# Products of seven-product row-tile pairs interleaved with those of the next pair, in a hybrid attention and FFN block

## The chip, the core and the metric

The kernel runs on one core of a Trainium2 chip. Its engines run side by side, each in the order of its own instruction list: PE (matrix multiply, into PSUM), DVE (elementwise), ACT (elementwise and activation functions), POOL (little used here) and SP, whose list here holds nothing but DMA issues. They meet at semaphores only. The metric is the device time of one execution in microseconds; less is better. The kernel before takes 1153.43 us, the median of three executions (1153.13, 1153.43, 1155.93).

## The reference

One transformer block over 256 positions of width 2048, all in float32. Four kinds of token mixing share one input projection; then comes the feed-forward part, which the change is about:

```python
h = rms_norm(x, norm_mix_pre)
mix = hybrid_mixer(h, ...)                 # retention, SSD scan, two attentions
x = x + rms_norm(mix @ w_out, norm_mix_post)
h = rms_norm(x, norm_ffn_pre)
f = (jax.nn.silu(h @ w_gate) * (h @ w_up)) @ w_down      # 2048 -> 5632 -> 2048
x = x + rms_norm(f, norm_ffn_post)
```

## The kernel before

Float32 precision is had from a fast PE format by splitting each operand in two: `hi` is the operand rounded (an ACT cast, L767) and `lo` what is left (a DVE subtraction, L768). One product is then three matmuls of 128 x 128 by 128 x 512: hi by hi, hi by lo, lo by hi (`mm1`, L811 to L815; the line of a matmul tells which of the three it is). Activations are split once and stay in SBUF; weights stream in from HBM, and every 128 x 1024 piece of them costs one ACT cast and one DVE subtraction.

The feed-forward part has three stages. The first (`gemm`) computes the first 512 hidden columns in the plain way. The second, called the gate stage below, computes the other 10 blocks of 512 columns of `w_gate` and `w_up` together. The third, the down stage, does `w_down` in two passes q = 0 and 1, each with 22 units. A unit is a pair of row tiles of the weights (2 x 128 rows): in the gate stage 8 units make a block. A unit has a 2 x 2 arrangement of weights (a, b for the two column groups, rows 0 and 1) against a 2 x 2 arrangement of activations (two row tiles, two halves of the 256 positions). Plainly it takes eight products (`eight`). `seven` does it in seven by a Strassen-like scheme: it needs sums of the weights, `ta` (L824, 128 x 1024) and `tb` (L826 and L827, 128 x 512 each), and sums of the activations, made once and held (`cmb`). So a seven-product unit costs PE 21 matmuls in place of 24, and costs DVE and ACT more: its four weight operands are `w0` (as loaded), `wa` (from ta), `wc` (half a piece as loaded) and `wb` (from tb). `S_UNITS` and `S_DOWN` say which units are taken in seven: 3 of 8 in each gate block, 4 of 22 and 7 of 22 in the down stage. Each such unit is done whole before the next unit begins.

Results gather in PSUM, which has 8 banks: four in one pool (`ps_a`: m1, q5, m7, m6) and two and two in others (b2 and b3; b4 and b8). `sums` folds the four into two SBUF tiles when the last seven of a block is done, and `join` (L860 to L864) adds the other four at the block's end. Then ACT and DVE make silu(g) * v (L928, L929), the block of f. `turn` transposes it on PE (eight 128 x 128 transposes) and ACT copies it to SBUF (L897); `hidden` splits it for the down stage (tiles `fs`, and `cmb` for a unit taken in seven).

A scheduler reorders each engine's list when the program is built; the lists are fixed before the run. What paces them is in the pools: weights as loaded live in 5 buffers (`raw`, 512 KB each), their split parts in 4 `hi` and 4 `lo` buffers. SP issues a load when the buffer that it reuses has been read for the last time, and the loads stand in one list, so a late one holds up those behind it.

Of the kernel before, what the change touches and what calls it, by code (L numbers as in the profile page):

```python
# [33 lines left out]
CK = 2  # L34
FFB = FF // 512
FKT = FF // P

S_UNITS = (0, 2, 4)
S_DOWN = ((0, 1, 5, 8), (0, 1, 3, 5, 7, 8, 10))
X_STEPS = [(0, 1), (1, 2), (2, 4), (4, 6), (6, 8), (8, 10), (10, 12), (12, 14), (14, 16)]  # L40


# [21 lines left out]
def _pack4(wa, wb, blocks, n_kt):  # L64


    parts = []
    for (ca, cb, n) in blocks:
        a, b = (w[:, c:c + n].reshape(n_kt // 2, 2, P, n) for w, c in ((wa, ca), (wb, cb)))
        q = np.stack([a[:, 0], b[:, 1], b[:, 0], a[:, 1]], axis=2)  # L70
        parts.append(np.ascontiguousarray(q).reshape(-1))
    return np.concatenate(parts)

# [26 lines left out]
def block_kernel(ctx: ExitStack, tc: tile.TileContext, I, out):  # L100
# [15 lines left out]
    def T(shape, name, dt=F32):  # L116

        count["t"] += 1
        return big.tile(shape, dt, tag="t", name=f"{name}_{count['t']}")
# [662 lines left out]
        split_to(o[:, 0], o[:, 1], s)  # L782
        return o

    def load4(src, i):

        n = 4 * P * 512
        w = src[i * n:(i + 1) * n].rearrange("(p c n) -> p c n", p=P, c=4)
        out = []
        for k in range(2):  # L790
            raw = wp.tile([P, CK * 512], F32, tag="raw", bufs=5, name="raw")
            r3 = raw.rearrange("p (c n) -> p c n", c=CK)
            nc.sync.dma_start(r3, w[:, 2 * k:2 * k + 2, :])
# [26 lines left out]
    def seven(m, src, i, x, u, cmb, last):  # L820

        ad, bc_ = load4(src, i)
# [8 lines left out]
        s = lambda j: [cmb[:, i, j, :] for i in range(2)]  # L831
        for name, (xa, xb), (hi, lo), k in (
                ("m1", xpart(x, u, 0, 0), w0, 0), ("b3", s(3), w0, 1), ("q5", s(0), wa, 0), ("m7", s(2), wa, 1),
                ("b2", xpart(x, u, 1, 0), wc, 0), ("m6", s(1), wb, 0), ("b4", xpart(x, u, 1, 1), wb, 1)):
            mm1(m, name, xa, xb, hi[:, k, :], lo[:, k, :], last and name[0] != "b")

    def eight(m, src, i, x, u, last=False, halves=(0, 1), ws=None):

        if ws is None:
            ws = [split_new(v) for v in load4(src, i)]  # L840
        (w0, w1) = ws
        for h in halves:
            for name, k, (hi, lo), j in (("b2" if h == 0 else "b4", 0, w0, 0), ("b3" if h == 0 else "b8", 1, w0, 1),
                                         ("b3" if h == 0 else "b8", 0, w1, 0), ("b2" if h == 0 else "b4", 1, w1, 1)):
                end = last and (name, j) in (("b3", 0), ("b8", 0), ("b2", 1), ("b4", 1)) and w1 is ws[1] and j + k == (
                    0 if name in ("b3", "b8") else 2)
                mm1(m, name, *xpart(x, u, k, h), hi[:, j, :], lo[:, j, :], end)
        return ws
# [19 lines left out]
    def combine_hs(u):  # L868
# [6 lines left out]
    accs = [[accps(f"ff{h}{i}") for i in range(2)] for h in range(2)]  # L875
    gemm(hs, [I["w_g"], I["w_u"]], [fr[0], fr[0]], 512, KT, accs, 4, (2, 3, 4, 7),
         {1: lambda: gained(1, 0), 2: lambda: gained(1, 1), 3: lambda: gained(1, 2), 4: lambda: gained(1, 3),
          5: lambda: [x_norm(h) for h in range(2)], 6: lambda: combine_hs(S_UNITS[0]),
          8: lambda: combine_hs(S_UNITS[1]), 9: lambda: combine_hs(S_UNITS[2])})
    for h in range(2):  # L880
        spill(h)
    sg = []
# [7 lines left out]
    def turn(b, f):  # L890

        ft.append(T([P, 4, S], f"ft{b}"))
        for h in range(2):
            ps = ps_c.tile([P, 512], F32, tag="b", name=f"fT{b}{h}")
# [15 lines left out]
    for b in range(1, FFB):  # L910
        m = {}
        g, v = T([P, 2, 512], "g"), T([P, 2, 512], "v")
        for u in range(KT // CK):
            i = (b - 1) * (KT // CK) + u
            if u in S_UNITS:
                seven(m, I["w_gu"], i, hs, u, cmb[u], u == S_UNITS[-1])
            else:
                eight(m, I["w_gu"], i, hs, u, u == KT // CK - 1)
            if u == 0:
                turn(b - 1, f)  # L920
            if u == S_UNITS[-1] + 1:
# [13 lines left out]
    for q in range(2):  # L935
# [103 lines left out]
```

## Time and profile before

| | |
|---|---|
| median of three executions | 1153.43 us |
| the profiled execution | 1157.54 us |
| its span on the core | 1155.6 us |
| PE busy in the span | 1123.8 us, 97% |
| DVE busy | 865.6 us, 75% |
| ACT busy | 613.1 us, 53% |
| granted TensorE clock, mean of the span | 0.996 |
| HBM, mean of the span | 193 GB/s |

The span is what the trace covers; the execution has 1.9 us around it. A matmul's duration in the trace is its time through the pipeline (0.39 us), while the next one starts after 0.23 us; so PE's busy share counts overlaps once, hides a short pause, and says little on how near PE is to its pace. The distance between the starts of matmuls tells that. For DVE and ACT too, a row's duration is a little longer than the distance to the next start. In a row of the timeline, the bracket at the end has the engine's idle time just before the instruction and what ended it.

### The profile page before, as it was taken

To read this page: it belongs to the slowest core of one execution; us is meant where nothing else is said; L and a number is where in the kernel's file an instruction comes from. 1 tells how busy PE (TensorE), PEld (TensorE's weight loads), DVE (VectorE), ACT (ScalarE), POOL (GpSimd) and SP (SyncE) were. 2 spreads that over 40 slices of the span, in tenths; PEclk is the share of its full clock that TensorE was granted. 3 is DMA by queue.
4 is the path that set the end of the run, shared out by engine and by line. 5 is a ranking of instruction groups with operands and counts; after the bars stand their busy time and mean duration, and the time that the engine had idled before them with its cause. 6 is when DMAs were issued, how large, how long until landed. Compare 5 with 4: busy or idle time off the path is not lost. (4 is left out here: it accounts for less than half of the span.)

```text
span 1155.6 us, 14581 instructions
## 1 busy us (share of the span) xinstructions
PE 1123.8 (97%) x5341; PEld 928.8 (80%) x5341; DVE 865.6 (75%) x1185; ACT 613.1 (53%) x846; POOL 14.2 (1%) x37
## 2 busy tenths in 40 slices
PE   9999999999999999999999999999999999989996
PEld 7787888888888887887787787787788788868885
DVE  5556647777565577898898897887898988479845
ACT  6644435565444475655555555555565666355532
POOL 0000000000000010000000000000000000000000
PEclk9999999999999999999999999999999999999998
DMA  8964454564456676556556556456456556546654
GB/s 275 317 227 146 142 155 124 185 208 162 153 188 192 213 266 204 182 195 205 181 186 204 176 196 204 164 199 206 164 196 215 192 194 218 194 153 216 221 196 150
DMA packets 65447, 224.35 MB, mean 194 GB/s; under 512 B 8032, under 2 KB 8544, under 8 KB 65376
## 3 DMA queue, kind: packets, MB, share of 16 engines
q1 hardware_dynamic: 65232, 223.42, 57.9%
q8 instruction: 42, 0.69, 0.2%
q14 instruction: 29, 0.24, 0.1%
q10 hardware_dynamic: 144, 0.01, 0.0%
HBM read 219.20 MB, written 4.19 MB: 193 GB/s over the span
## 5 line engine op out<-in xcount | busy, mean ns | idle before, releaser
L767 ACT CAST hi<-raw 128x1024 fp32r<-128x1024 f32 x248 | 238.6, 980 | 205.9 <-PE b L815 180.8
L768 DVE TENSOR_TENSOR lo<-raw,hi 128x1024 fp32r<-128x1024 f32 x248 | 277.6, 1133 | 67.4 <-ACT hi L767 63.5
L182 DVE TENSOR_TENSOR lo<-raw,hi 128x1024 fp32r<-128x1024 f32 (+3 forms) x154 | 175.5, 1154 | 115.9 <-ACT hi L181 115.4
L181 ACT CAST hi<-raw 128x1024 fp32r<-128x1024 f32 (+3 forms) x154 | 150.7, 994 | 129.9 <-PE wo L199 32.1
L814 PE MATMUL b<-lo,hs 128*128 128x512 f32 x460 | 180.3, 392 | 0.3 <-DVE lo L768 0.3
L813 PE MATMUL b<-hi,hs 128*128 128x512 f32 x460 | 180.1, 392 | 0.0
L815 PE MATMUL b<-hi,hs 128*128 128x512 f32 x460 | 179.2, 390 | 0.0
L814 PE MATMUL b<-lo,fs 128*128 128x512 f32 x286 | 111.7, 391 | 0.3 <-DVE lo L768 0.3
L815 PE MATMUL b<-hi,fs 128*128 128x512 f32 x286 | 111.4, 390 | 0.0
L813 PE MATMUL b<-hi,fs 128*128 128x512 f32 x286 | 110.7, 390 | 0.1
L814 PEld LDWEIGHTS b<-lo,hs 128*128 128x128 f32 x460 | 86.4, 188 | 18.4 <-DVE lo L768 1.0
L813 PEld LDWEIGHTS b<-hi,hs 128*128 128x128 f32 x460 | 86.4, 188 | 17.8
L815 PEld LDWEIGHTS b<-hi,hs 128*128 128x128 f32 x460 | 86.4, 188 | 17.6
L824 DVE TENSOR_TENSOR ta<-raw 128x1024 f32<-128x1024 f32 x41 | 50.1, 1223 | 30.6 <-DMA raw<-in_w_gu 29.2
L814 PEld LDWEIGHTS b<-lo,fs 128*128 128x128 f32 x286 | 53.8, 188 | 12.6 <-DVE lo L768 1.4
L813 PEld LDWEIGHTS b<-hi,fs 128*128 128x128 f32 x286 | 53.7, 188 | 11.9 <-ACT hi L767 0.7
L768 DVE TENSOR_TENSOR lo<-tb,hi 128x1024 fp32r<-128x1024 f32 x41 | 50.1, 1222 | 17.1 <-ACT hi L767 17.1
L815 PEld LDWEIGHTS b<-hi,fs 128*128 128x128 f32 x286 | 53.8, 188 | 11.1
L767 ACT CAST hi<-tb 128x1024 fp32r<-128x1024 f32 x41 | 43.1, 1052 | 28.9 <-DVE lo L768 13.0
L767 ACT CAST hi<-ta 128x1024 fp32r<-128x1024 f32 x41 | 43.2, 1054 | 26.0 <-PE b L815 17.4
L768 DVE TENSOR_TENSOR lo<-ta,hi 128x1024 fp32r<-128x1024 f32 x41 | 50.0, 1219 | 0.1
L196 PE MATMUL wo<-hi,ms 128*128 128x512 f32 x128 | 50.0, 390 | 0.0
(378 smaller groups left out, 2025.8 us busy)
## 6 DMA issues: line engine op xcount, KB each, us to landing
raw<-in_w_gu SPq DMA_DIRECT2D x160, 512.0 KB, 4.5
raw<-in_w_down SPq DMA_DIRECT2D x88, 512.0 KB, 4.2
raw<-in_w_in SPq DMA_DIRECT2D x78, 512.0 KB, 4.5
raw<-in_w_out SPq DMA_DIRECT2D x32, 512.0 KB, 3.5
raw<-in_w_in SPq DMA_DIRECT2D x16, 384.0 KB, 3.1
raw<-in_w_g SPq DMA_DIRECT2D x8, 512.0 KB, 4.8
raw<-in_w_u SPq DMA_DIRECT2D x8, 512.0 KB, 4.7
raw<-in_w_in SPq DMA_DIRECT2D x8, 264.0 KB, 2.8
```

The lines of the kernel that those rows point to most:

```text
L181: nc.scalar.copy(hi[:, k, :n], r3[:, k, :])
L182: nc.vector.tensor_tensor(lo[:, k, :n], r3[:, k, :], hi[:, k, :n].bitcast(F32), ALU.subtract)
L196: nc.tensor.matmul(d[:, :n], lhsT=a, rhs=hi[:, kt % CK, :n], start=first, stop=False)
L767: nc.scalar.copy(hi, v)
L768: nc.vector.tensor_tensor(lo, v, hi.bitcast(F32), ALU.subtract)
L813: nc.tensor.matmul(o, lhsT=xa, rhs=hi, start=first, stop=False)
L814: nc.tensor.matmul(o, lhsT=xa, rhs=lo, start=False, stop=False)
L815: nc.tensor.matmul(o, lhsT=xb, rhs=hi, start=False, stop=last)
L824: nc.vector.tensor_tensor(ta, ad, bc_[:, 0:1, :].to_broadcast([P, 2, 512]), ALU.add)
```

## The change

`seven` is replaced by `fifteen`, which takes a unit u in seven and the next one, u + 1, in eight, with their 15 products interleaved: two of the seven (w0), four of the eight (its first piece, w0e), two of the seven (wa), four of the eight (w1), three of the seven (wc, wb). The tables now name the first unit of each such pair: units 1, 3 and 5 of a gate block with their partners 2, 4 and 6, so that a block begins with unit 0 and ends with unit 7, both plain. In the down stage the pairs start at 3, 7, 11, 15 (q = 0) and 1, 3, 5, 7, 9, 11, 15 (q = 1). As many units as before are taken in seven. The weights of all units are packed in another order (a0, b0, b1, a1), so a unit taken in eight is still loaded in runs of 4 KB per partition (two adjacent columns of 512), and one taken in seven in two runs of 2 KB per load (a0 with b1, b0 with a1). `turn` moves from after a block's first unit to the block's end, and takes its two PSUM banks from `ps_a`; `hidden` runs up to two units ahead; `sums` follows the last pair directly.

```diff
-S_UNITS = (0, 2, 4)
-S_DOWN = ((0, 1, 5, 8), (0, 1, 3, 5, 7, 8, 10))
+S_UNITS = (1, 3, 5)
+S_DOWN = ((3, 7, 11, 15), (1, 3, 5, 7, 9, 11, 15))
...
-        q = np.stack([a[:, 0], b[:, 1], b[:, 0], a[:, 1]], axis=2)
+        q = np.stack([a[:, 0], b[:, 0], b[:, 1], a[:, 1]], axis=2)
...
+    def eight(m, src, i, x, u, last=False, halves=(0, 1), ws=None):
+        if ws is None:
+            ws = [split_new(v) for v in load4(src, i, slice(0, 2), slice(2, 4))]
+        for h in halves:
+            n0, n1 = ("b2", "b3") if h == 0 else ("b4", "b8")
+            for name, k, w, j in ((n0, 0, 0, 0), (n1, 0, 0, 1), (n1, 1, 1, 0), (n0, 1, 1, 1)):
...
+    def fifteen(m, src, i, x, u, cmb, last, end=False):
...
+        ad, bc_ = load4(src, i, slice(0, 3, 2), slice(1, 4, 2))
         ta, tb = T([P, 2, 512], "ta"), T([P, 2, 512], "tb")
         nc.vector.tensor_tensor(ta, ad, bc_[:, 0:1, :].to_broadcast([P, 2, 512]), ALU.add)
+        r0, r1 = load4(src, i + 1, slice(0, 2), slice(2, 4))
         w0 = split_new(ad)
+        prod(("m1", xpart(x, u, 0, 0), w0, 0), ("b3", s(3), w0, 1))
+        w0e = split_new(r0)
         nc.vector.tensor_tensor(tb[:, 0, :], ta[:, 0, :], ad[:, 1, :], ALU.add)
         nc.vector.tensor_tensor(tb[:, 1, :], tb[:, 0, :], bc_[:, 1, :], ALU.add)
+        part8(w0e)
         wa = split_new(ta)
+        w1 = split_new(r1)
+        prod(("q5", s(0), wa, 0), ("m7", s(2), wa, 1))
+        part8(w1)
         wc = split_new(bc_[:, 1:2, :])
         wb = split_new(tb)
+        prod(("b2", xpart(x, u, 1, 0), wc, 0), ("m6", s(1), wb, 0), ("b4", xpart(x, u, 1, 1), wb, 1))
...
             if u in S_UNITS:
-                seven(m, I["w_gu"], i, hs, u, cmb[u], u == S_UNITS[-1])
-            else:
+                fifteen(m, I["w_gu"], i, hs, u, cmb[u], u == S_UNITS[-1], u == KT // CK - 2)
+            elif u - 1 not in S_UNITS:
                 eight(m, I["w_gu"], i, hs, u, u == KT // CK - 1)
-            if u == 0:
-                turn(b - 1, f)
-            if u == S_UNITS[-1] + 1:
+            if u == 4 and b == FFB - 1:
+                hidden(0)
+            if u == S_UNITS[-1]:
                 sums(m, g, v)
...
+        turn(b - 1, f)
...
         for u in range(n_u):
-            hidden(u)
...
-            if q == 0 and u == 1:
+            if q == 0 and u == 0:
                 turn(FFB - 1, f)
+            for k in (u + 1, u + 2):
+                if k < n_u:
+                    hidden(k)
```

The first place is DVE's list in the fourth gate block, around the end of a unit taken in seven. Before (from the second seven of the block; `ta_184`, `tb_185` are its sums, `ta_186` is the next seven's, the `lo` of raw 5425 and 5427 belong to the plain unit between them):

```order
L768 TENSOR_TENSOR lo_5393<-ta_184_5383,hi_5392 128x1024
L827 TENSOR_TENSOR tb_185_5384<-tb_185_5384,raw_5381 128x512
L768 TENSOR_TENSOR lo_5397<-raw_5381,hi_5396 128x512
L824 TENSOR_TENSOR ta_186_5465<-raw_5461,raw_5463 128x1024
L768 TENSOR_TENSOR lo_5401<-tb_185_5384,hi_5400 128x1024
L768 TENSOR_TENSOR lo_5430<-raw_5425,hi_5429 128x1024
L768 TENSOR_TENSOR lo_5434<-raw_5427,hi_5433 128x1024
L768 TENSOR_TENSOR lo_5469<-raw_5461,hi_5468 128x1024
```

Now (the first fifteen of the block, from the `lo` of w0e; `ta_183` is the next pair's):

```order
L769 TENSOR_TENSOR lo_5339<-raw_5323,hi_5338 128x1024
L855 TENSOR_TENSOR tb_182_5321<-ta_181_5320,raw_5316 128x512
L769 TENSOR_TENSOR lo_5357<-ta_181_5320,hi_5356 128x1024
L856 TENSOR_TENSOR tb_182_5321<-tb_182_5321,raw_5318 128x512
L769 TENSOR_TENSOR lo_5361<-raw_5325,hi_5360 128x1024
L769 TENSOR_TENSOR lo_5385<-raw_5318,hi_5384 128x512
L850 TENSOR_TENSOR ta_183_5406<-raw_5402,raw_5404 128x1024
L769 TENSOR_TENSOR lo_5389<-tb_182_5321,hi_5388 128x1024
L769 TENSOR_TENSOR lo_5414<-raw_5402,hi_5413 128x1024
```

In both lists the next `ta` stands right ahead of the `lo` of the unit's own `tb`; what moved is the plain unit's splitting, which now stands inside the unit, ahead of that `ta`, and not behind it.

The second place is DVE's list where the down stage goes from q = 0 to q = 1 (`v` and `g` join the PSUM banks of q = 0, `oe` is its output part, `ta_293` the first sum of q = 1). Before, with unit 0 of q = 1 taken in seven:

```order
L768 TENSOR_TENSOR lo_8766<-raw_8758,hi_8765 128x1024
L861 TENSOR_TENSOR v_275_8256<-b3_250_7807,v_275_8256 128x512
L860 TENSOR_TENSOR g_274_8255<-g_274_8255,b2_250_7819 128x512
L949 TENSOR_TENSOR oe00_290_8740<-v_275_8256,g_end0_248_7776 128x512
L949 TENSOR_TENSOR oe00_290_8740<-g_274_8255,g_end0_248_7776 128x512
L864 TENSOR_TENSOR v_275_8256<-v_275_8256,b8_254_7920 128x512
L863 TENSOR_TENSOR g_274_8255<-g_274_8255,b4_250_7827 128x512
L949 TENSOR_TENSOR oe10_291_8749<-v_275_8256,g_end0_248_7776 128x512
L949 TENSOR_TENSOR oe10_291_8749<-g_274_8255,g_end0_248_7776 128x512
L824 TENSOR_TENSOR ta_293_8762<-raw_8758,raw_8760 128x1024
```

Now, with unit 0 plain and the first pair at unit 1 (the first two rows split unit 0's weights):

```order
L769 TENSOR_TENSOR lo_8763<-raw_8758,hi_8762 128x1024
L769 TENSOR_TENSOR lo_8767<-raw_8760,hi_8766 128x1024
L877 TENSOR_TENSOR v_285_8540<-b3_243_7775,v_285_8540 128x512
L876 TENSOR_TENSOR g_284_8539<-g_284_8539,b2_243_7771 128x512
L963 TENSOR_TENSOR oe00_290_8740<-v_285_8540,g_end0_243_7757 128x512
L963 TENSOR_TENSOR oe00_290_8740<-g_284_8539,g_end0_243_7757 128x512
L880 TENSOR_TENSOR v_285_8540<-v_285_8540,b8_243_7789 128x512
L879 TENSOR_TENSOR g_284_8539<-g_284_8539,b4_243_7785 128x512
L963 TENSOR_TENSOR oe10_291_8749<-v_285_8540,g_end0_243_7757 128x512
L963 TENSOR_TENSOR oe10_291_8749<-g_284_8539,g_end0_243_7757 128x512
L769 TENSOR_TENSOR lo_8810<-raw_8798,hi_8809 128x1024
L850 TENSOR_TENSOR ta_293_8802<-raw_8798,raw_8800 128x1024
```

The `ta` stays behind the eight joining instructions; what moved ahead of them is a whole plain unit's splitting.

The third place is ACT's list at the start of the down stage, where `fs` of unit 1 is first needed. Before (`fs_245` is unit 1's, `g_236` the last gate block, `ft10` its transposed form):

```order
L767 CAST fs_245_7719<-ft0_156_4267 128x2x256
L767 CAST cmb_247_7727<-cs_246_7722 128x512
L767 CAST hi_7734<-raw_7730 128x1024
L767 CAST hi_7738<-raw_7732 128x1024
L767 CAST hi_7785<-raw_7778 128x1024
L767 CAST hi_7791<-ta_249_7782 128x1024
L928 ACTIVATE g_236_7409<-g_236_7409,rsf0_r_3999 128x512
```

Now (`ft9` is the block before the last, `g_233` the last gate block, raw 7873 and 7875 the weights of unit 2, `fs_245` again unit 1's):

```order
L912 COPY ft9_242_7734<-fT91_142_7741 128x4x128
L942 ACTIVATE g_233_7398<-g_233_7398,rsf0_r_3999 128x512
L942 ACTIVATE g_233_7398<-g_233_7398,rsf1_r_4014 128x512
L768 CAST hi_7877<-raw_7873 128x1024
L768 CAST hi_7881<-raw_7875 128x1024
L912 COPY ft10_244_7799<-fT100_143_7800 128x4x128
L912 COPY ft10_244_7799<-fT101_144_7806 128x4x128
L768 CAST fs_245_7812<-ft0_160_4545 128x2x256
L768 CAST cmb_247_7820<-cs_246_7815 128x512
```

`fs_245` moved from ahead of the last block's silu to behind it, behind unit 2's casts and behind both copies of the last transposes.

## Rows read from the trace of the kernel before

**Rows 1.** The page's first line:
```profile
span 1155.6 us, 14581 instructions
```
**Rows 2.** Windows: gate stage, q = 0, q = 1; window and length, busy by engine, clock, DMA:
```profile
465.41:904.17 438.76, 427.48 (x1911) 349.99 (x1910) 377.40 (x433) 242.20 (x272) 0.00 (x0) 1.00 0.58 193
904.17:1023.92 119.75, 119.23 (x525) 97.20 (x524) 89.29 (x104) 67.38 (x85) 0.00 (x0) 1.00 0.56 189
1023.92:1145.21 121.29, 117.60 (x508) 95.71 (x506) 89.46 (x96) 58.83 (x66) 0.81 (x2) 0.99 0.57 193
```
**Rows 3.** Timeline of PE, an undisturbed stretch; start, duration, instruction:
```profile
487.12 0.39 PE L813 MATMUL m<-hi,hs 128*128 128x512 f32 x1
...
497.10 0.39 PE L815 MATMUL b<-hi,hs 128*128 128x512 f32 x1
```
**Rows 4.** Timeline of PE around the two transpose groups of a block:
```profile
469.95 0.39 PE L815 MATMUL b<-hi,hs 128*128 128x512 f32 x1
...
472.22 0.39 PE L815 MATMUL b<-hi,hs 128*128 128x512 f32 x1
```
**Rows 5.** Waits of PE from 465 to 1146 us: total, times, longest:
```profile
PE m L814 <- DVE lo L768: 11.0, 8, 1.7
```
**Rows 6.** Timeline of PE at one of the eight waits:
```profile
566.62 0.39 PE L813 MATMUL m<-hi,cmb 128*128 128x512 f32 x1
568.30 0.50 PE L814 MATMUL m<-lo,cmb 128*128 128x512 f32 x1 [1.29 <-DVE lo L768]
```
**Rows 7.** Timeline of DVE in the same stretch:
```profile
561.99 0.69 DVE L827 TENSOR_TENSOR tb<-tb,raw 128x512 f32<-128x512 f32 x1
562.59 0.29 DVE L777 TENSOR_TENSOR cs<-ft 128x128 f32<-128x128 f32 x1
...
565.88 1.23 DVE L824 TENSOR_TENSOR ta<-raw 128x1024 f32<-128x1024 f32 x1 [1.66 <-DMA raw<-in_w_gu]
567.02 1.22 DVE L768 TENSOR_TENSOR lo<-tb,hi 128x1024 fp32r<-128x1024 f32 x1
```
**Rows 8.** Landing of weight loads: issued 465 to 900, at 561.0, at 569.4:
```profile
DMA to landing us min/median/max: 3.1/4.5/7.4
DMA to landing us min/median/max: 4.8/4.8/4.8
DMA to landing us min/median/max: 3.3/3.3/3.3
```
**Rows 9.** Waits of DVE from 465 to 1146 us:
```profile
DVE ta L824 <- DMA raw<-in_w_gu: 29.2, 18, 2.7
```
**Rows 10.** Timeline of ACT and DVE at a block's end:
```profile
682.91 0.72 ACT L928 ACTIVATE g<-g,rsf_r 128x512 f32<-128x512 f32 x1 [2.88 <-DVE g L860]
683.67 0.75 DVE L929 SCALAR_TENSOR_TENSOR v<-v,rsf_r,g 128x512 f32<-128x512 f32 x1 [0.79 <-ACT g L928]
```
**Rows 11.** Timeline of DVE, then of PE, where q = 1 begins:
```profile
1020.73 0.69 DVE L861 TENSOR_TENSOR v<-b,v 128x512 f32<-128x512 f32 x1 [1.09 <-PE b L815]
1026.12 1.23 DVE L824 TENSOR_TENSOR ta<-raw 128x1024 f32<-128x1024 f32 x1
1028.53 0.50 PE L813 MATMUL q<-hi,cmb 128*128 128x512 f32 x1 [3.08 <-ACT hi L767]
```
**Rows 12.** Windows: just behind that wait:
```profile
1028.50:1033.45 4.95, 4.40 (x11) 3.18 (x12) 4.95 (x6) 2.93 (x4) 0.00 (x0) 0.66 0.67 207
```
**Rows 13.** Timeline of ACT in q = 0:
```profile
914.35 0.62 ACT L767 CAST fs<-ft 128x512 fp32r<-128x512 f32 x1
914.87 1.04 ACT L767 CAST hi<-raw 128x1024 fp32r<-128x1024 f32 x1
915.82 0.58 ACT L897 COPY ft<-fT 128x512 f32<-128x512 f32 x1
916.29 1.05 ACT L767 CAST hi<-raw 128x1024 fp32r<-128x1024 f32 x1
```
**Rows 14.** The page's DMA issues: line, count, size, median time to landing:
```profile
xr<-in_x SPq DMA_DIRECT2D x4, 512.0 KB, 8.3
```

More of the change, by code (lines that the diff above doesn't have):

```diff
@@ L783, in combine, with load4 @@
         return o
-    def load4(src, i):
+    def load4(src, i, *parts):
         n = 4 * P * 512
@@ L789, in load4 @@
         out = []
-        for k in range(2):
+        for k in parts:
             raw = wp.tile([P, CK * 512], F32, tag="raw", bufs=5, name="raw")
-            r3 = raw.rearrange("p (c n) -> p c n", c=CK)
-            nc.sync.dma_start(r3, w[:, 2 * k:2 * k + 2, :])
+            v = w[:, k, :]
+            r3 = raw[:, :v.shape[1] * 512].rearrange("p (c n) -> p c n", c=v.shape[1])
+            nc.sync.dma_start(r3, v)
             out.append(r3)
@@ L818, in xpart @@
         return [x[u][:, k, i, h * P:(h + 1) * P] for i in range(2)]
-    def seven(m, src, i, x, u, cmb, last):
-        ad, bc_ = load4(src, i)
+    def eight(m, src, i, x, u, last=False, halves=(0, 1), ws=None):
[4 more added lines that the diff above has]
+            for name, k, w, j in ((n0, 0, 0, 0), (n1, 0, 0, 1), (n1, 1, 1, 0), (n0, 1, 1, 1)):
+                hi, lo = ws[w]
+                mm1(m, name, *xpart(x, u, k, h), hi[:, j, :], lo[:, j, :], last and w == 1)
+        return ws
@@ new lines, in fifteen, with prod, part8 @@
+    def fifteen(m, src, i, x, u, cmb, last, end=False):
+        s = lambda j: [cmb[:, i, j, :] for i in range(2)]
+        def prod(*items):
+            for name, (xa, xb), (hi, lo), k in items:
+                mm1(m, name, xa, xb, hi[:, k, :], lo[:, k, :], last and name[0] != "b")
+        def part8(w):
+            k = 0 if w is w0e else 1
+            for h in range(2):
+                names = ("b2", "b3") if h == 0 else ("b4", "b8")
+                for j in range(2):
+                    mm1(m, names[j ^ k], *xpart(x, u + 1, k, h), w[0][:, j, :], w[1][:, j, :], end and k == 1)
+        ad, bc_ = load4(src, i, slice(0, 3, 2), slice(1, 4, 2))
@@ L828, in seven @@
         wa = split_new(ta)
+        w1 = split_new(r1)
+        prod(("q5", s(0), wa, 0), ("m7", s(2), wa, 1))
+        part8(w1)
         wc = split_new(bc_[:, 1:2, :])
         wb = split_new(tb)
[L831 to L848, printed above, removed]
+        prod(("b2", xpart(x, u, 1, 0), wc, 0), ("m6", s(1), wb, 0), ("b4", xpart(x, u, 1, 1), wb, 1))
@@ L877, in block_kernel @@
          {1: lambda: gained(1, 0), 2: lambda: gained(1, 1), 3: lambda: gained(1, 2), 4: lambda: gained(1, 3),
-          5: lambda: [x_norm(h) for h in range(2)], 6: lambda: combine_hs(S_UNITS[0]),
-          8: lambda: combine_hs(S_UNITS[1]), 9: lambda: combine_hs(S_UNITS[2])})
+          5: lambda: [x_norm(h) for h in range(2)], **{c: (lambda u=u: combine_hs(u)) for c, u in zip((6, 8, 9, 10), S_UNITS)}})
     for h in range(2):
@@ L893, in turn @@
         for h in range(2):
-            ps = ps_c.tile([P, 512], F32, tag="b", name=f"fT{b}{h}")
+            ps = accps(f"fT{b}{h}")
             for j in range(4):
@@ L915, in block_kernel @@
             if u in S_UNITS:
-                seven(m, I["w_gu"], i, hs, u, cmb[u], u == S_UNITS[-1])
-            else:
+                fifteen(m, I["w_gu"], i, hs, u, cmb[u], u == S_UNITS[-1], u == KT // CK - 2)
+            elif u - 1 not in S_UNITS:
                 eight(m, I["w_gu"], i, hs, u, u == KT // CK - 1)
-            if u == 0:
-                turn(b - 1, f)
-            if u == S_UNITS[-1] + 1:
+            if u == 4 and b == FFB - 1:
+                hidden(0)
+            if u == S_UNITS[-1]:
                 sums(m, g, v)
-            if u == 6 and b >= FFB - 2:
-                hidden(b - FFB + 2)
+        turn(b - 1, f)
         for h in range(2):
@@ L952, in block_kernel @@
         for u in range(n_u):
-            hidden(u)
             i = q * n_u + u
             if u in S_DOWN[q]:
-                seven(m, I["w_down"], i, fs, u, fcmb[u], u == S_DOWN[q][-1])
+                fifteen(m, I["w_down"], i, fs, u, fcmb[u], u == S_DOWN[q][-1])
+            elif u - 1 in S_DOWN[q]:
+                pass
             elif u < n_u - skew:
@@ L960, in block_kernel @@
                 held[u] = eight(m, I["w_down"], i, fs, u, u == n_u - 1, halves=(0,))
-            if q == 0 and u == 1:
+            if q == 0 and u == 0:
                 turn(FFB - 1, f)
-            if u == S_DOWN[q][-1] + 1:
+            for k in (u + 1, u + 2):
+                if k < n_u:
+                    hidden(k)
+            if u == S_DOWN[q][-1]:
                 g, v = T([P, 2, 512], "g"), T([P, 2, 512], "v")
```

## The prediction

> **What bounds the kernel now.** I read the page's first line, then the windows by stage, then PE's timeline for its pace, then who made PE wait, and last the lists of the engines it waited for. The span is 1155.6 us [rows 1] and the execution around it 1157.54 us, 4.1 us above the median of the runs shown. All sums below are made against the span; I take the same number off the median.
>
> PE is the bound, and the reader should see how close it is to its own pace. In an undisturbed stretch 44 matmuls pass from 487.12 to 497.10 us [rows 3]: 0.2267 us each, at the full clock. The transposes of one block lie in a stretch of 2.27 us with six matmul steps (1.36 us) [rows 4], so they cost 0.91 us. By the code the gate stage has 10 blocks of 61 products, 1830 matmuls; q = 0 has 172 products (516 matmuls) and q = 1 has 169 (507). At pace, with transposes in ten blocks and once in q = 0:
> - gate stage: 1830 x 0.2267 + 10 x 0.91 = 424.0 us; it took 438.8 [rows 2]: 14.8 over.
> - q = 0: 117.0 + 0.9 = 117.9; it took 119.75: 1.9 over.
> - q = 1: 114.9; it took 121.3: 6.4 over, of which 0.2 is the last matmul's way through the pipeline: 6.2.
>
> That is 22.9 us in which PE lost its pace, 2% of the time, though PE counts as 97% busy. Nothing else in these stages can be won, since the change leaves the number of matmuls as it is.
>
> Where it goes: eight waits of PE on a `lo`, 11.0 us [rows 5]. One of them, by starts: 566.62 to 568.30 is 1.68 us where 0.23 is normal, so it costs 1.45 [rows 6]. The `lo` that was late is the one of `tb`. It is late because DVE stood 1.66 us at the `ta` ahead of it, waiting for a load [rows 7]. DVE had 18 such waits, 29.2 us [rows 9]; eight reached PE. So the true releaser is a load that came too late, through a queue: the load was issued at 561.0, as soon as the buffer's last reader (the first half of tb) was done, and landed 4.8 us later [rows 8], while DVE had only some 3.3 us of other work before it wanted it.
>
> In q = 1 there is one wait of 3.08 us [rows 11], on the first `wa`. DVE began to join q = 0 at 1020.73 and came to `ta` at 1026.12, behind eight joining instructions; PE, with unit 0 in seven, wanted wa after only two products. The granted clock behind it is 0.66 over 4.95 us [rows 12], 1.2 GHz for part of it: 11 matmuls where 22 go at pace.
>
> **Part by part.** Distances between starts are the prices: on DVE 1.14 us for 128 x 1024 and 0.60 for 128 x 512 [rows 7]; on ACT 0.95 for a cast of 1024, 0.47 for a copy, 0.52 for a cast of 512 [rows 13].
>
> *Interleaving.* A seven takes DVE four operations of 1.14 (ta, w0, wa, wb) and three of 0.60: 6.4 us, against 21 x 0.2267 = 4.8 on PE. An eight takes 2.3 against 5.4. So DVE falls behind by 1.6 in each seven and gains 3.1 in each eight. A fifteen takes the sum, 8.6 against 10.2: DVE is ahead in every pair, and inside it the products alternate. DVE's total does not change (377 us of 439 [rows 2]); only its place does.
>
> *The load behind the wait.* The next `ta` still stands ahead of this unit's `lo` of tb, so the head of the queue can still block. But its second load now reuses the buffer of w0e. Between that buffer's last read and the next `ta`, DVE has tb, wa, tb, w1, wc: 0.60 + 1.14 + 0.60 + 1.14 + 0.60 = 4.1 us, and by the walk below the load before it left over 8 us earlier, so it flies alone: 3.3 us, as the one issued at 569.4 did [rows 8]. For the third pair the distance is about 4.6. So I expect `ta` to wait little or nothing. If it does, there is slack: I walk DVE through a block's end from the start of the transposes (0), where unit 7's last banks are done at 0.2. Unit 7's second piece can be cast when w1's buffer is free, three products of the pair and eight of unit 7 before 0 (11 x 0.68 = 7.5, less 0.2 in the pipeline: -7.3), and is cast by -6.2. Then DVE splits three pieces and makes four sums (3 x 1.14 + 4 x 0.60 = 5.8), to -0.3; four joins end at 2.2, ta 3.4. On ACT the cast of w0e waits for unit 7's end (0.3 to 1.25), two copies follow to 2.2, two silu of 0.72 [rows 10] to 3.6; DVE's products with them take 0.75 at most [rows 10] and end at 4.8. Then w0 5.9, w0e 7.0, wa 8.8, w1 10.5, wc 11.1, ta 12.3, wb 13.4. PE does the transposes to 0.9, unit 0 to 6.35, and wants the `lo` of w0 at 6.6, w0e 7.9, wa 10.6, w1 12.0, wb 15.4. Everything is in time, by 0.7 us at the tightest (w0) and by 2.0 for wb. So the second load may take 6.1 us before PE feels it; 4.5 is the median so far and 7.4 the longest [rows 8].
>
> *2 KB runs.* A seven's loads now come in twice as many pieces. The trace has no such load of 512 KB. From below: nothing, 3.3 us alone; a gain cannot come from smaller pieces. From above: 8.3 us, the slowest 512 KB load of the page [rows 14]. I take 3.4, by the lone load, as half of the loads only change their source columns.
>
> *Transposes.* They cost 0.91 before and after. At the block's end they wait for nothing: f of the block before is 40 us old. They even give DVE time to join before b2 is reused. Cost 0.
>
> *Start of q = 1.* Unit 0 is plain now, so wa is wanted 5.4 + 6 x 0.68 = 9.5 us after the start, not 1.4. By DVE's list (join done 1.4 us after, then w0, ta, w0e, tb, wa) it is ready at 7.2. The wait goes, and with it the low clock. I leave 0.5 us for late operands: 5.7 gained.
>
> *Start of q = 0: a new wait.* `fs` of unit 1 now stands on ACT behind unit 2's casts, which wait for unit 0's last product, and behind two copies. From the start of the transposes before unit 0: unit 0 ends at 6.35; the cast of unit 2's second piece runs 6.65 to 7.6, the copies to 8.55, fs to 9.1 [rows 13]. PE wants it at 6.35 + 0.91 = 7.25: 1.9 us waiting, with nothing to hide it. With 0.2 of old unevenness, q = 0 stays 2.1 over where it was 1.9: 0.2 lost. Would the clock fall behind this wait? The eight waits of up to 1.7 us did not lower it: the gate stage reads 1.00 [rows 2]; the one of 3.08 did [rows 12]. I take no fall. [...]
>
> *Gate stage.* Of the 14.8 the eight waits explain some 12: 8 x 1.45. I let 2.0 stay, as an estimate from that rest of 3: unevenness that no wait explains, and 0.1 per block for things not seen. Gained: 12.8.
>
> Sum: 12.8 - 0.2 + 5.7 = 18.3 us. The part before 465 us and the last 10 us after PE's end are the same instructions. 1153.4 - 18.3 = 1135.1 us, and about 1139 for a profiled execution. The floor is 1153.4 - 22.9 = 1130.5.
>
> **Rivals.**
> 1. *The wait moves to the block's start.* The tightest margin is 0.7 us for w0, behind joins, silu and ACT's copies. If that chain is 1.5 us longer (say the silu waits, as DVE did for 0.79 [rows 10], twice), each of 10 blocks loses 0.8: 1143. For it: ten instructions on two engines in a row. Against it: ta now fills the time of the silu.
> 2. *The queue's head still blocks.* `ta` ahead of wb keeps its place. If loads land 1 us above the longest margin (7.1 us) in all 20 places of the gate stage where a pair follows a pair, 20 us come back: 1153, no change; in a third of them, 1142. For it: 7.4 has been seen. Against it: that was with several in flight.
> 3. *The new wait lowers the clock.* Ten matmuls at 0.43 in place of 0.23: 2 us, 1137.
> 4. *Slower: loads in 2 KB runs.* The mechanism is the chain load, ta, wb, w0, next load. Above 6.1 us per landing PE waits for the difference in 25 places (20 in the gate stage, 5 in q = 1). It decides at 6.1 + 18.3 / 25 = 6.8 us: above that the kernel is slower than before. At 8.3 us: 25 x 2.2 = 55 lost, 18 won, 1190. Against it: HBM traffic stays 193 GB/s, 58% of the queues' time [rows 2], and doubling the pieces would have to double the landing.
> 5. *It does nothing*, if the waits are DVE's total work and not its order: then the 15 us reappear somewhere. Against it: 377 us of 439 [rows 2] leaves DVE 14% idle.
>
> **How the numbers follow.** Forecast 0.68 (1131 to 1139), rival 1 0.08, rival 3 0.10, rival 2 0.07 (half of it under 0.3%), rival 4 0.04, rival 5 0.03. A difference under 0.3% (3.5 us) can't be told from none here. Faster: 0.68 + 0.08 + 0.10 + 0.04 = 0.90 (the 0.04 is rival 2's larger half); same: 0.03 + 0.03 = 0.06; slower 0.04. The range for 8 in 10 goes from the floor to rival 1: 1130.5 to 1144.
>
> **What would show it.** Gate blocks of 42.4 to 42.7 us from block to block where they took 43.9; no wait of PE on the `lo` of tb; DVE's wait for loads at ta well under 29 us; a wait of about 1.9 us of PE on `fs` near 898 us; none at the start of q = 1, and the clock at 1.00 there. Wrong would be: landings over 6 us for the split loads, a wait in each block at w0 or w0e, or a clock under 1.00 in the gate stage.

## Result

The changed kernel took 1137.14 us (median of 4 runs, 1134.34 to 1139.61) against 1153.89 us of the kernel before (4 runs, 1153.13 to 1155.93): a ratio of 0.9851, 95% interval 0.9825 to 0.9878. Run again (experiment 9) it took 1135.54 against 1155.13 us (ratio 0.9838, 0.9822 to 0.9853). The forecast was 1135.1 in a range of 1130.5 to 1144.0, and it held. By stage, in spans of the profiled executions (forecast: the stage before less its term):

| stage | before, us | forecast | after | after, second profile |
|---|---|---|---|---|
| up to the gate stage | 465.4 | 465.4 | 464.5 | 463.8 |
| gate stage | 438.8 | 426.0 | 423.8 | 423.8 |
| q = 0 | 119.8 | 120.0 | 121.7 | 120.1 |
| q = 1 | 121.3 | 115.6 | 115.1 | 115.1 |
| span | 1155.6 | 1137.3 | 1135.4 | 1133.1 |

The spans differ by 20.2 us, the medians by 16.8. The profiled execution of before was 3.7 us above the median of its runs, and the part up to the gate stage, the same work in all, takes 461.8 to 465.4 us from one profile of a kernel with five load buffers to the next. What follows goes by stages. In the two profiles of the kernel after, the gate stage and q = 1 repeat to 0.1 us and q = 0 does not (121.7 and 120.1); of the kernel before there is one profile, so how well its stages repeat is not shown.

### The profile page after: what moved, and what is told of

Its sections match the earlier page's. It is cut to its first block, busy times and chain, and to the rows that moved or that the text cites. A ratio compares the mean times of both kernels' runs of the same rounds, so it can differ in the third digit from the quotient of the medians.

```text
span 1135.4 us, 14600 instructions
## 1 busy us (share of the span) xinstructions
PE 1118.2 (98%) x5341; PEld 932.1 (82%) x5341; DVE 863.9 (76%) x1185; ACT 613.5 (54%) x846; POOL 14.2 (1%) x37
## 4 chain that ended last, share of the span: by engine, by line
PE 91%; DVE 3%; DMA 3%; ACT 2%; issue 1%; POOL 0%; SPq 0%; DVEq 0%; POOLq 0%; ACTq 0%
PE b L815 15%; PE b L817 15%; PE b L816 15%; PE sx L223 3%; PE wo L197 3%; PE wo L198 3%; PE wo L200 3%; PE m L817 2%; PE m L815 2%; PE m L816 2%; PE dk L223 2%; PE lk L223 2%; PE rqk L223 2%; PE dq L223 2%; DMA raw<-in_w_in 2%; PE lq L223 1%
## 5 line engine op out<-in xcount | busy, mean ns | idle before, releaser
L768 ACT CAST hi<-raw 128x1024 fp32r<-128x1024 f32 x248 | 242.0, 983 | 173.6 <-PE b L817 143.6
```

Of the source, the lines that this page charges most:

```text
L768: nc.scalar.copy(hi, v)
```

## The profile after

First the page's first line and one of its groups (line, engine, operation, tiles, count; busy us and mean ns; idle time before them and what ended most of it). DVE stood idle 4.3 us in total ahead of the `ta` additions of all 41 pairs, 4.1 of it for loads of `w_gu`, where those had cost 29.2 in 18 places [rows 9]:

```profile
span 1135.4 us, 14600 instructions
L850 DVE TENSOR_TENSOR ta<-raw 128x1024 f32<-128x1024 f32 x41 | 49.9, 1216 | 4.3 <-DMA raw<-in_w_gu 4.1
```

The windows of the gate stage, q = 0 and q = 1, columns as in [rows 2]. PE's busy time now equals the length of the first and the last but for hundredths, at a clock of 1.00; only q = 0 has a gap:

```profile
464.51:888.28 423.77, 423.77 (x1912) 351.67 (x1910) 370.13 (x420) 240.41 (x268) 0.00 (x0) 1.00 0.62 199
888.28:1009.94 121.66, 119.86 (x528) 98.92 (x526) 95.99 (x118) 70.54 (x91) 0.00 (x0) 0.99 0.61 196
1009.94:1125.03 115.09, 115.08 (x508) 94.97 (x506) 88.52 (x95) 57.72 (x65) 0.82 (x2) 1.00 0.60 197
```

Two block ends on PE's timeline (start, duration, instruction). From the first transposes to the second it is 42.40 us; 183 matmuls of 0.2267 and 0.91 of transposes are 42.40. At PE's pace nothing is left to win in a block:

```profile
548.37 1.04 PE L911 MATMUL fT<-ident,v 128*128 128x128 f32 x8
...
590.77 1.03 PE L911 MATMUL fT<-ident,v 128*128 128x128 f32 x8
```

Of PE's waits from the gate stage on (total, times, longest), where there had been eight on `lo` and the 3.08 us of q = 1 [rows 5, 11], beside three of 0.3 to 0.5 us, one row stands:

```profile
PE b L815 <- ACT fs L768: 1.8, 1, 1.8
```

It is the wait the prediction computed from ACT's list. ACT's timeline shows the two casts for unit 2, the two copies and then `fs`:

```profile
892.73 1.05 ACT L768 CAST hi<-raw 128x1024 fp32r<-128x1024 f32 x1 [1.79 <-issue]
894.09 1.05 ACT L768 CAST hi<-raw 128x1024 fp32r<-128x1024 f32 x1 [0.31 <-PE b L817]
895.05 1.06 ACT L912 COPY ft<-fT 128x512 f32<-128x512 f32 x2
896.00 0.63 ACT L768 CAST fs<-ft 128x512 fp32r<-128x512 f32 x1
```

and PE's timeline shows what stood behind it: 1.8 us idle, about 1.4 us at pace, then starts 0.43 us apart where 0.23 is normal, until 901.6. The last line is the window over that stretch: clock 0.67, so 1.2 GHz for part of it.

```profile
893.85 1.03 PE L911 MATMUL fT<-ident,v 128*128 128x128 f32 x8
896.68 0.50 PE L815 MATMUL b<-hi,fs 128*128 128x512 f32 x1 [1.80 <-ACT fs L768]
897.02 0.39 PE L816 MATMUL b<-lo,fs 128*128 128x512 f32 x1
...
898.66 0.63 PE L816 MATMUL b<-lo,fs 128*128 128x512 f32 x1
899.09 0.63 PE L817 MATMUL b<-hi,fs 128*128 128x512 f32 x1
...
901.82 0.39 PE L815 MATMUL b<-hi,fs 128*128 128x512 f32 x1
```

```profile
896.50:901.60 5.10, 4.92 (x15) 3.88 (x16) 4.94 (x8) 2.73 (x6) 0.00 (x0) 0.67 0.66 203
```

The walk of DVE through a block's end can be checked on its timeline. From the transposes at 548.37 the forecast had the joins end at 2.2 us, `ta` at 3.4, the products with silu at 4.8, w0e at 7.0, wa at 8.8. Start plus duration gives 2.1, 3.2, 4.5, 6.8 and 8.5:

```profile
549.76 0.68 DVE L880 TENSOR_TENSOR v<-v,b 128x512 f32<-128x512 f32 x1
550.36 1.22 DVE L850 TENSOR_TENSOR ta<-raw 128x1024 f32<-128x1024 f32 x1
551.50 1.40 DVE L943 SCALAR_TENSOR_TENSOR v<-v,rsf_r,g 128x512 f32<-128x512 f32 x2
552.82 2.35 DVE L769 TENSOR_TENSOR lo<-raw,hi 128x1024 fp32r<-128x1024 f32 x2
555.10 0.68 DVE L855 TENSOR_TENSOR tb<-ta,raw 128x512 f32<-128x512 f32 x1
555.70 1.21 DVE L769 TENSOR_TENSOR lo<-ta,hi 128x1024 fp32r<-128x1024 f32 x1
```

## Experiments

Experiments 1 to 4 shared one chip and the runs of before (median 1155.92 us), 5 to 8 the same chip later (1156.83), 9 to 11 another chip (1155.13). Each row is from the one profiled execution of its kernel.

### Is it the lateness of the load, or its place ahead of lo?

The theory has two halves: the load is late, and `ta`, waiting for it, stands ahead of the `lo` that PE needs. Experiment 3 was to mend the first half alone.

```
-            raw = wp.tile([P, CK * 512], F32, tag="raw", bufs=5, name="raw")
+            raw = T([P, CK * 512], "rawt") if spare and not k else wp.tile([P, CK * 512], F32, tag="raw", bufs=5, name="raw")
...
-        ad, bc_ = load4(src, i)
+        ad, bc_ = load4(src, i, src is I["w_gu"])
```

> The kernel before, and in the gate stage the first of a seven's two loads goes into a tile of the large pool, so that the five raw buffers serve three loads per pair of units in place of four. DVE's list keeps ta ahead of the lo of tb in every block. My theory: the wait came from a load that left too late because its buffer came free too late; with buffers to spare ta does not wait, the eight PE waits on lo<-tb go, the gate stage falls from 438.8 to 425 to 428 us, q = 1 stays at 121: about 1141 in all. Rival: the order itself (a seven's DVE work, 6.4 us against 4.8 on PE) is what makes lo late; DVE no longer waits for loads but the PE waits stay, the gate stage 436 to 439, no change of time.

It came out slower than before, 1171.26 us (ratio 1.0138, 1.0123 to 1.0153). The window of the gate stage, then DVE's and PE's rows in it:

```profile
463.73:916.70 452.97, 439.18 (x1912) 345.14 (x1910) 375.66 (x432) 240.34 (x271) 0.00 (x0) 1.00 0.56 186
```

```profile
DVE ta L824 <- DMA rawt<-in_w_gu: 41.7, 10, 5.2
```

```profile
PE m L813 <- ACT hi L767: 6.0, 9, 0.8
PE q L813 <- ACT hi L767: 4.7, 9, 0.5
PE b L813 <- ACT hi L767: 2.2, 10, 0.2
PE m L814 <- DVE lo L768: 0.8, 1, 0.8
```

Neither side was met. The waits inside the blocks went but for one of 0.8 us, but at ten block starts the loads left in a bunch (five within 4.5 us around 558, landing in up to 7.6), and `ta` waited 4.2 us each on average. PE's waits in the rows above add up to 13.7 us, while the stage lies 29 over its pace; the rest is not traced. Moving a buffer to another pool also moved when its load leaves. Experiment 5 gives the loads their lead without that, with one more buffer in the same ring (the number changes in all four places that name the ring):

```
-            raw = wp.tile([P, CK * 512], F32, tag="raw", bufs=5, name="raw")
+            raw = wp.tile([P, CK * 512], F32, tag="raw", bufs=6, name="raw")
...
-    t2p = ctx.enter_context(tc.tile_pool(name="t2p", bufs=4))
+    t2p = ctx.enter_context(tc.tile_pool(name="t2p", bufs=2))
```

> The kernel before with six raw buffers in place of five (the small pool t2p has two buffers in place of four to make room, which touches the part before the gate stage). DVE's list keeps ta ahead of the lo of tb in nine blocks, loads go through the same queue in the same order, only each may leave one buffer earlier. My theory (a load that leaves too late, behind which lo is queued): DVE's waits at ta fall from 29.2 to under 8 us, the PE waits on lo<-tb go, the gate stage falls from 438.8 to 424 to 428 us; q = 1 stays near 121. Rival (the order alone, DVE's 6.4 us per seven against 4.8 on PE): PE waits stay and the gate stage is 436 to 439. The run before this one of this kind moved the load into another pool and made it later, so it could not tell these apart.

1142.25 us (ratio 0.9878, 0.9864 to 0.9893). Gate stage and q = 1, then DVE's waits in the gate stage; PE has none there:

```profile
463.60:888.03 424.43, 424.43 (x1911) 350.65 (x1910) 376.43 (x425) 243.07 (x273) 0.00 (x0) 1.00 0.61 200
...
1006.64:1130.46 123.82, 118.86 (x508) 95.08 (x506) 89.69 (x96) 58.93 (x66) 0.82 (x2) 0.99 0.56 184
```

```profile
DVE ta L824 <- DMA raw<-in_w_gu: 8.2, 13, 1.3
```

One buffer takes 14.3 of the 14.8 us. The scheduler made DVE's list anew, but the third seven's `ta` still stands ahead of the `lo` of the second seven's `tb`: in all ten blocks where it was nine, and mostly with two instructions between them where there was none. DVE still waits 13 times, 0.6 us each, and PE feels none of it. q = 1 keeps its wait and gets a second one of 1.5 us on a `lo`: it is 2.5 us longer than before.

The other half, order alone, was tried twice. Experiment 4 held every `ta` behind the `lo` of the unit ahead of it:

```
-        nc.vector.tensor_tensor(ta, ad, bc_[:, 0:1, :].to_broadcast([P, 2, 512]), ALU.add)
+        late(nc.vector.tensor_tensor(ta, ad, bc_[:, 0:1, :].to_broadcast([P, 2, 512]), ALU.add))
```

> The kernel before with ta held at its place in the program on DVE: behind the lo of the unit ahead of it, and so never ahead of the lo of the last tb. Buffers and loads as before. My theory: with nothing that can wait for a load ahead of it, the lo of tb is in time; the eight PE waits go even though the loads leave no earlier: gate stage 425 to 430, time 1141 to 1145. Rival: ta, now 3.4 us later in DVE's list, makes the lo of wa late instead; 0.5 to 1.1 us in each of 30 sevens, gate stage 440 to 458, as slow as before or slower.

1201.93 us (ratio 1.0402, 1.0388 to 1.0415). Gate stage and PE's waits in it:

```profile
465.19:942.58 477.39, 444.90 (x1911) 358.19 (x1910) 386.43 (x437) 243.50 (x274) 0.00 (x0) 0.96 0.55 178
```

```profile
PE q L813 <- ACT hi L767: 32.0, 10, 3.3
```

The rival's wait, on `wa`, but in ten places and not in thirty: at the blocks' starts, where the hold also put `ta` behind the joins and silu of the block before. No row on `lo` of `tb` is left. So experiment 6 held `ta` only inside the blocks of the gate stage:

```
-        nc.vector.tensor_tensor(ta, ad, bc_[:, 0:1, :].to_broadcast([P, 2, 512]), ALU.add)
+        t = nc.vector.tensor_tensor(ta, ad, bc_[:, 0:1, :].to_broadcast([P, 2, 512]), ALU.add)
+        if x is hs and u > 0:
+            late(t)
```

> The kernel before with ta held behind the lo of the unit ahead of it in the gate stage, but only for the second and third seven of a block; the first, at the block's start, and all of the down stages stay as before. My theory: the earlier run with this hold paid its 46 us at the blocks' starts alone; inside the blocks the wait on lo<-tb had gone. So here the eight waits go and nothing comes in their place: gate stage 425 to 428 us, 11 to 14 us faster than before. Rival: the hold makes wa late inside the blocks as well: gate stage 438 or more.

1143.31 us (ratio 0.9887, 0.9872 to 0.9902); PE has no wait in the gate stage, and DVE's row for `ta` is close to that of experiment 5:

```profile
464.52:888.70 424.18, 424.18 (x1912) 350.97 (x1910) 377.90 (x432) 242.05 (x271) 0.00 (x0) 1.00 0.61 199
```

```profile
DVE ta L824 <- DMA raw<-in_w_gu: 8.4, 8, 1.4
```

Did each edit take away one half and leave the other? The traces tell, for the third seven's second load, its `ta`, and the `lo` of the second seven's `tb`: medians of the ten blocks, in us from the start of the block's first transposes:

| | load leaves | lands | DVE free for `ta` | `ta` starts | `lo` of `tb` starts |
|---|---|---|---|---|---|
| before | 4.2 | 9.0 | 6.8 | 9.1 | 10.2 |
| experiment 5 | 1.0 | 6.0 | 5.6 | 6.1 | 8.4 |
| experiment 6 | 4.1 | 8.7 | 11.6 | 11.6 | 7.7 |

In experiment 5 the load comes 3 us earlier and `ta` keeps its place; in experiment 6 the load comes about as late as before and `ta` has left its place. So both halves are needed for the loss: take away either one, the late load or its place ahead of `lo`, and the gate stage runs at pace. The rival that DVE's work as such is the bound has fallen: it was the same in both (376 and 378 us, 377 before).

### How much lead does the interleaving give?

Experiment 11 takes one buffer from the kernel after, in all four places that name the ring; one of them:

```
-            raw = wp.tile([P, CK * 512], F32, tag="raw", bufs=5, name="raw")
+            raw = wp.tile([P, CK * 512], F32, tag="raw", bufs=4, name="raw")
```

> The kernel after with four raw buffers in place of five. My theory: the change works because a load's buffer comes free earlier before it is wanted; taking one buffer away takes that lead back: each load leaves some 4 us later, DVE waits 1 to 3 us at ta in two of three pairs, and PE waits on lo<-tb or hi<-ta again: gate stage 430 to 450 us against 423.8, time 1145 to 1165. Rival: the alternation of the products alone gives the gain, and DVE has 14% idle to take the later loads in: gate stage 424 to 426, no change.

1156.45 us (ratio 1.0010, 0.9997 to 1.0024): the whole gain is gone. Gate stage, then PE's waits in it:

```profile
469.97:907.35 437.38, 429.07 (x1912) 350.18 (x1910) 370.76 (x420) 237.33 (x269) 0.00 (x0) 1.00 0.59 193
```

```profile
PE m L816 <- DVE lo L769: 7.2, 9, 1.5
PE b L816 <- DVE lo L769: 0.9, 3, 0.4
```

The gate stage gives back 13.6 us, but not by the waits of before, and not by those expected. The nine waits of the first row are on the `lo` of `w0`, at the first pair of nine of the ten blocks: the place where the prediction's walk had its smallest margin (0.7 us), and that of its rival 1. The block at 600 us shows how. The load of `w0e`, issued at 595.39, landed 6.0 us later; ACT stood at its cast, with two copies and the two silu behind it; DVE's products with silu waited for those, and the `lo` of `w0` stands behind the products. PE waited 1.45 us for it at 606.77:

```profile
601.49 1.05 ACT L768 CAST hi<-raw 128x1024 fp32r<-128x1024 f32 x1 [3.00 <-DMA raw<-in_w_gu]
604.16 1.41 DVE L943 SCALAR_TENSOR_TENSOR v<-v,rsf_r,g 128x512 f32<-128x512 f32 x2 [2.35 <-ACT g L942]
605.50 2.35 DVE L769 TENSOR_TENSOR lo<-raw,hi 128x1024 fp32r<-128x1024 f32 x2
```

```profile
ACT hi L768 <- DMA raw<-in_w_gu: 54.0, 21, 3.3
```

In the gate stage of the kernel after ACT waits for no load at all. So the cause is again a late load at the head of an in-order list, now ACT's in place of DVE's. The part ahead of the gate stage also loses 5 to 8 us by the missing buffer, while q = 1 keeps its gain (115.8 us). In time, the interleaving is worth about one load buffer in the gate stage, as experiment 5 found from the other side; the lists differ in more than that, for the scheduler made them anew.

### What is the interleaving's, and what the new beginning's?

Experiment 2 is the kernel before with the new tables, and the transposes at the block's end (behind the loop over u, their tiles from `ps_a`), without interleaving:

```
-S_UNITS = (0, 2, 4)
-S_DOWN = ((0, 1, 5, 8), (0, 1, 3, 5, 7, 8, 10))
+S_UNITS = (1, 3, 5)
+S_DOWN = ((3, 7, 11, 15), (1, 3, 5, 7, 9, 11, 15))
...
-            if u == 0:
-                turn(b - 1, f)
...
+        turn(b - 1, f)
```

> The kernel before with the new tables of units (blocks and q = 1 begin with a plain unit) and the transposes at the block's end, but with a seven and the eight behind it done one after the other, not interleaved. My theory: the interleaving gives the gate stage's gain and the plain beginning that of q = 1. DVE's list still has the next ta ahead of the lo of the second seven's tb in nine blocks of ten, so the gate stage stays near 438 us (436 to 441) with PE waits on lo<-tb; q = 1 falls from 121.3 to about 115.5. Time about 1148 (1146 to 1150). Rival: the plain beginning alone gives DVE its lead; the gate stage falls to 424 to 426 and the time to 1134 to 1137.

1148.71 us (ratio 0.9942, 0.9928 to 0.9956). The time is as expected, its parts less so. The three stages, then PE's waits in the first and in the last:

```profile
461.82:894.90 433.08, 427.81 (x1911) 350.21 (x1910) 375.05 (x426) 241.79 (x271) 0.00 (x0) 1.00 0.59 194
894.90:1015.62 120.72, 118.60 (x528) 97.72 (x526) 92.79 (x112) 68.61 (x88) 0.00 (x0) 1.00 0.59 200
1015.62:1134.07 118.45, 116.22 (x508) 94.60 (x506) 88.36 (x95) 57.70 (x65) 0.81 (x2) 1.00 0.57 189
```

```profile
PE m L814 <- DVE lo L768: 5.0, 6, 1.8
PE m L814 <- DVE lo L768: 2.2, 3, 1.0
```

The gate stage gained 5.7 us where I expected 436 to 441, near 438.8, and q = 1 gained 2.8 of 6.2. In this profile the gate stage's waits on `lo` of `tb` stay, but are fewer and on average shorter; whether the new tables or the new place of the transposes did that is not separated. In q = 1 the wait at its beginning has gone, and three on the `lo` of `tb`, behind a `ta` that waits for its load, have come. Interleaving, with `hidden` running ahead, which was not tested alone, then brings the other 9.3 us of the gate stage and 3.4 of q = 1. The profiled execution was 1.9 us under the median of its runs, so the split is good to about 2 us.

### The parts costed at nothing

Experiment 7 puts the transposes back behind unit 0 of the next block, in the kernel after:

```
+            if u == 0:
+                turn(b - 1, f)
...
-        turn(b - 1, f)
```

> The kernel after with the transposes back behind unit 0 of the next block, as they stood before the change. My theory: they cost the same 0.9 us there, but at the block's end they also covered the join of b2: DVE frees b2 at about 548.6 us where PE's last product starts at 548.1, and unit 0, now plain, writes b2 first. PE waits 0.3 us for b2 and 0.2 for b3 at each of 10 block starts: gate stage 423.8 + 3 to 5 = 427 to 429 us, time up 3 to 5 us against the kernel after. Rival: nothing waits, since PE is behind DVE: within 1 us of the kernel after.

1141.64 us, beside 1136.29 of experiment 8 on the same chip, which is the kernel after in all but a packing. The gate stage, and PE's timeline at a block's start:

```profile
464.92:894.61 429.69, 426.92 (x1912) 351.03 (x1910) 372.80 (x423) 238.76 (x270) 0.00 (x0) 1.00 0.62 197
```

```profile
550.34 0.39 PE L817 MATMUL b<-hi,hs 128*128 128x512 f32 x1
551.01 0.47 PE L815 MATMUL b<-hi,hs 128*128 128x512 f32 x1 [0.28 <-DVE g L876]
```

A start 0.67 us behind the one before, where 0.23 is normal, ten times, on the join of b2: 4.4 of the 5.9 us that the stage lost (the other 1.5 are not traced). At the block's end the transposes are work that PE has to do anyway, put where it would wait.

Experiment 8 packs the weights of the sevens so that each load is one 4 KB run per partition:

```
+        for u in us:
+            q[u] = np.stack([a[u, 0], b[u, 1], b[u, 0], a[u, 1]], axis=1)
...
-        ad, bc_ = load4(src, i, slice(0, 3, 2), slice(1, 4, 2))
+        ad, bc_ = load4(src, i, slice(0, 2), slice(2, 4))
```

> The kernel after, but the weights of the units taken in seven are packed so that each load of theirs is one run of 4 KB per partition again, not two of 2 KB. Same order of instructions. My theory: the 2 KB runs cost nothing here; landings and the one DVE wait at ta stay, the time is within 1 us of the kernel after, the gate stage 423.8. Rival: 2 KB runs land slower by some tenths; the median landing of the gate stage's loads falls by 0.3 us or more, with no change of time, since nothing waits for them.

1136.29 us (ratio 0.9830, 0.9809 to 0.9851) and a gate stage of 423.80: no difference. A seven's second load, which flies nearly alone, landed in 3.6 us in 2 KB runs (kernel after, issued at 648.2) and 3.2 in 4 KB runs (this kernel, at 646.5), with like medians at all three places of a block (3.57 to 3.70 against 3.18 to 3.30). Over all loads of the stage the median is 4.7 and 4.4 us, so the rival of this run is what came: they land slower by some tenths, and nothing waits for them. The forecast took 3.4. The rows of those two loads, after first:

```profile
DMA to landing us min/median/max: 3.6/3.6/3.6
```

```profile
DMA to landing us min/median/max: 3.2/3.2/3.2
```

### The wait that is left

Experiment 1 records the split of unit 1's activations in the last gate block:

```
-            if u == 4 and b == FFB - 1:
-                hidden(0)
+            if u in (2, 4) and b == FFB - 1:
+                hidden(u // 2 - 1)
```

> The kernel after, with the split of unit 1's activations (fs of unit 1) recorded in the last gate block beside that of unit 0, no longer behind unit 2's casts and the two copies. My theory: the one PE wait left in the kernel after (1.8 us on fs, at 896.68 us) goes, and with it the eight matmuls at 0.43 us behind it; q = 0 shrinks from 121.7 us to about 118.0, and the time falls 3.6 us, to about 1133.5. Rival A: the wait only moves to the fs of unit 2, which stands behind the same copies: q = 0 stays at 121 to 122 us, no change. Rival B: the slow stretch comes from the transposes in front of it and not from the wait: q = 0 shrinks by 1.8 us only.

1133.66 us (ratio 0.9809, 0.9796 to 0.9821), the fastest kernel here. From the gate stage on PE waits for nothing; gate stage and q = 0:

```profile
463.74:887.51 423.77, 423.77 (x1911) 351.78 (x1910) 371.91 (x426) 241.14 (x270) 0.00 (x0) 1.00 0.62 199
887.51:1005.49 117.98, 117.98 (x527) 97.80 (x526) 93.83 (x112) 69.52 (x89) 0.00 (x0) 1.00 0.62 203
```

Experiments 9 and 10 put the kernel after, unchanged, and this one side by side.

> The kernel after, unchanged, beside the next two on one chip. My theory of its one wait (1.8 us on fs where q = 0 begins): the wait comes in every execution, the slow stretch behind it only in some: in the profiled executions of three kernels with this same wait so far, it came once (q = 0 took 121.7 us) and twice not (120.0 us). So q = 0 here is 120.0 or 121.7 us, nothing between, and the median 1135 to 1138. Rival: the slow stretch belongs to this kernel's place of the transposes and comes every time: 121.7.

> The kernel with the split of unit 1's activations in the last gate block, again, on the same chip as the kernel after. My theory: no PE wait from the gate stage on, q = 0 118.0 us; 2.0 us faster than the kernel after where its clock holds and 3.7 where it falls, so 2 to 4 in the median, with less scatter. Rival: less than 1 us, the wait being regained by other work.

The kernel after took 1135.54 us (1133.79 to 1138.32), with q = 0 at 120.08; the stretch behind the wait ran at full clock:

```profile
887.55:1007.63 120.08, 118.28 (x528) 97.82 (x527) 95.93 (x118) 70.53 (x91) 0.00 (x0) 1.00 0.62 199
895.78:900.88 5.10, 4.92 (x22) 4.06 (x23) 4.94 (x8) 3.22 (x7) 0.00 (x0) 1.00 0.64 202
```

The other took 1134.28 us (1133.03 to 1135.27; ratio to before 0.9822, 0.9809 to 0.9835), with q = 0 again 117.98. By the profiles it is 2.1 us better in that stage; by the medians only 1.3, less than the 2 to 4 expected, and the two intervals overlap. Its scatter was smaller each time (2.4 and 2.2 us from the fastest to the slowest run, against 4.5 and 5.3 of the kernel after).

## Why the prediction was right

- **Gate stage** (forecast 12.8 gained, measured 15.0). The mechanism was right in both halves (experiments 5 and 6). The term let 2.0 us stay as unevenness that no wait explains; nothing stayed. That rest seems to have had the same cause, for it also went where one buffer or the order alone was changed (424.4 and 424.2 us, experiments 5 and 6).
- **The second load flies alone in 3.4 us**: 3.6. **2 KB runs at most a little**: 0.4 us for each such load, felt by nobody. Rival 4, with its 6.8 us, was far off.
- **Transposes at 0**: right, and the reason given, that they cover the join of b2, was right too (experiment 7: 5.9 us without it).
- **q = 1** (5.7 forecast): 6.2. The half microsecond kept for late operands was not needed. The term spoke of the beginning alone, and that was too simple: the plain beginning takes its wait away, but without interleaving other waits follow in the stage, and only 2.8 is left (experiment 2).
- **q = 0, the new wait**: 1.9 us computed, 1.8 measured. The choice "I take no fall" of the clock was wrong for the execution profiled first: rival 3, given 0.10, came about there and cost 1.6 us (121.66 against 120.08). It was right in the four other profiles with this wait. So the term of 0.2 us for q = 0 measured 1.9 in the first profile and 0.3 in the second.
- **Rivals 1, 2 and 5** fell: nothing waits at the blocks' starts, where the walk was right to 0.3 us; `ta` at the head of the queue waited once, in the first block, for 3.6 us, and PE did not feel it; and the change did something, where rival 5 had it do nothing. Rival 1 had the right place to fear: with one load buffer less the waits come there (experiment 11).
- The sum: 15.0 - 1.9 + 6.2 + 0.9 (the part ahead, by chance) = 20.2 in the spans, against 18.3 forecast. That they are so near is in part luck: the gate stage and q = 1 gave 2.7 more than forecast, q = 0 lost 1.7 more, and 0.9 came by chance. Between the medians it is 16.8 in the first result, 19.6 in experiment 9 and 20.5 in experiment 8.

## What to carry to other kernels

When an engine waits on an operand, look at what stands ahead of that operand's producer in its in-order list: here the busy engine (DVE, 377 of 439 us) was not the bound, a late load at the head of its list was, and one more load buffer, a better order, or work interleaved so that buffers come free sooner each cured it. Try the buffer first, where there is room (here another pool gave up two of its own): it is the smallest edit, and taking one away from the tuned kernel shows how much lead an elaborate order really gives. An edit that moves when loads leave or where an instruction stands (another pool, a hold on an instruction) can cost more at a stage's edge than it saves inside, so hold it to the place where the wait was.

## What was not expected of the hardware

The same wait does not always cost the same. The 1.8 us on `fs` behind the transposes came in five profiled executions (the kernel after twice, experiments 7, 8 and 11); the granted clock fell behind it in one (0.67 over 5.1 us) and not in four (1.00 in experiment 9, above). The eight waits of up to 1.7 us in the gate stage of before [rows 5] had none: the 5.1 us behind each of them read 1.00. (The stage's mean of 1.00 [rows 2], on which the prediction leaned, could have hidden one fall.) In the first 20 us of two other profiled executions a fall did follow a wait of 1.5 to 1.6 us: experiments 10 and 11, at 13.2 and 12.8 us, with 0.67 and 0.70 over 5.1 us. The longer waits all had one: in the traces of all kernels there are 16 of 2.6 to 3.3 us (q = 1 of before [rows 12] and of experiments 3 to 6, and eleven where the blocks and q = 0 begin in experiment 4, whose gate stage reads 0.96), and the 5 us behind each read 0.50 to 0.66.

The Trainium skill ("TensorE: Matmul & The Clock Gate", section "Why this matters for your kernels") warns against long idle gaps between bursts of matmuls, because the clock goes back to its low level in them. The waits of 3.1 to 3.3 us agree. Its row is on longer gaps than the three of 1.5 to 1.8 us that had a fall here, and why those had one and the others not remains open.
